# The first RMSNorm of a hybrid encoder block: sums of squares from a second copy of x with tokens on partitions

## The chip, the cores and the metric

The kernel runs on one core of one Trainium2 chip. The metric is the device time of one execution in microseconds (us): 740.09 us, the median of 3 runs (740.04 to 740.13).

The engines go by their names in the profile: PE multiplies matrices, DVE works elementwise along partitions, ACT computes scaled copies, squares and table functions, POOL does a little setup, SP issues nearly all DMA transfers. Each engine works through its own list of instructions in order and waits where an operand or a buffer is not ready.

## The reference

One block over x of 512 tokens by 1024 channels, all in float32:

```
h = rms_norm(x, g_mix)                       # x * rsqrt(mean(x*x, channels) + 1e-6) * g
[u_a | u_b | gates] = h @ w_in               # 1024 -> 1280 + 1024 + 2048
A = (RG-LRU forward + backward of conv4(u_a)) @ p_a
B = (multi-scale mean pooling of u_b, per-group linear, scale) @ p_b
x = x + (sigmoid(g_a) * A + sigmoid(g_b) * B) @ w_out
up = conv3(rms_norm(x, g_ffn) @ w_up);  x = x + (gelu(gate) * val) @ w_down
out = rms_norm(x, g_final)
```

The change concerns only the first line: the factor 1/sqrt(mean of squares + eps) of each token.

## The kernel before

Activations lie with channels on the 128 partitions and the 512 tokens along the row, so x is fetched as eight tiles xt of 128 x 512 from a transposed copy xT. Each matrix product runs in three passes: weights and activations are split into a high part hi and a low part lo, and `mm` (lines 211 to 218) issues hi by hi, hi by low activations and low weights by hi: lines 216, 217 and 218 in the profile.

The weights come in chunks of eight 128 x 128 blocks (512 KB), in the order in which PE reads them. `need` (line 199) sees to it that chunk c is fetched (`fetch`, line 181, on SP) and cut (`cut`, line 189: the high half on ACT, line 192, the low half on DVE, line 193). There are four buffers each for the raw chunk, for its high half and for its low half, so a chunk waits for the chunk four places before it.

In the start stage PE works on the first seven output blocks of w_in at once, in seven PSUM banks st0 to st6: for each k of eight channel tiles it goes over the seven banks. Chunks 0 to 6 serve this stage; the last block of k = 6 is the first of chunk 6. The gain g_mix is multiplied in when x is split (line 226), and the token's factor 1/rms is applied to the finished products: every evacuation of a bank multiplies by the tile rstd1 (`evac`, line 361), in which all 128 partitions hold the same row of 512 factors.

The row comes about like this. ACT squares the eight xt tiles (`square`, line 326), DVE adds them up to ssq, still with channels on partitions. ssq is split, and `row_rstd` (line 232) multiplies it on PE by a matrix of ones: two matmuls (lines 235 and 236) behind k = 5, which sum over the partitions and leave the sum in each of them. ACT takes the square root (line 238) and DVE the reciprocal (line 239) of a 128 x 512 tile. The second norm uses the same helper.

In this stage the order on ACT, DVE and SP is that of the code (`pin` keeps it); PE's order, and what follows the stage, is set by a scheduler. Transfers on SP wait in order: at most eight are under way at a time, since each waits for the one eight places before it.

Of the kernel before, what the change touches and what calls it, by code (L numbers as in the profile page):

```python
# [9 lines left out]
F32 = mybir.dt.float32  # L10
F32R = mybir.dt.float32r
AF = mybir.ActivationFunctionType
ALU = mybir.AluOpType

P = 128
S = 512
D = 1024
KD = D // P
# [110 lines left out]


@with_exitstack
def block_kernel(ctx: ExitStack, tc: tile.TileContext, xT, fst, wts, cst, gfin, out):
    nc = tc.nc
    cp = ctx.enter_context(tc.tile_pool(name="cp", bufs=1))
    wp = ctx.enter_context(tc.tile_pool(name="wp", bufs=1))
# [3 lines left out]
    dp = ctx.enter_context(tc.tile_pool(name="dp", bufs=1, space=bass.MemoryType.DRAM))  # L139
# [4 lines left out]
    def T(dt=F32, name="t"):  # L144
        seq[0] += 1
        return up.tile([P, S], dt, tag="T", name=f"{name}_{seq[0]}", bufs=59)
# [5 lines left out]
    def PS(name="ps"):  # L152
        seq[0] += 1
        return psp.tile([P, S], F32, tag="ps", name=f"{name}_{seq[0]}", bufs=8)
# [3 lines left out]
    rstd1 = cp.tile([P, S], F32, tag="rstd", name="rstd1", bufs=1)  # L158
    eps = cp.tile([P, 1], F32, name="eps")
# [15 lines left out]
    ve = Pinned()  # L175

    def pin(ins):
        if pinned[0]:
            tc.keep_in_program_order(ins)

    def fetch(c):
        raws[c] = wp.tile([P, UNITS * P], F32, tag="raw", name=f"raw_{c}", bufs=4)
        pin(nc.sync.dma_start(raws[c], wts[c]))
# [5 lines left out]
    def cut(c):  # L189
        raw = raws.pop(c)  # L190
        halves(c)
        pin(nc.scalar.activation(his[c], raw, AF.Copy))  # L192
        pin(nc.vector.tensor_tensor(los[c], raw, his[c], op=ALU.subtract))  # L193
# [4 lines left out]
    def need(c, ahead=AHEAD):  # L198
        while fetched[0] < min(NCHUNK, c + 1 + ahead):
            fetch(fetched[0])  # L200
            fetched[0] += 1
        while ready[0] < min(NCHUNK, c + 1 + ahead):
            cut(ready[0])
            ready[0] += 1

    def unit(u):
        c, i = divmod(POS[u], UNITS)
        need(c, AHEAD if c >= NST else 0)
        s = slice(i * P, (i + 1) * P)
        return his[c][:, s], los[c][:, s]  # L210

    def mm(ps, u, x, start, stop, cols=slice(0, S)):
        wh, wl = unit(u)
        xh, xl = x[0][:, cols], x[1][:, cols]
        o = ps[:, cols]
        nc.tensor.matmul(o, wh, xh, start=start, stop=False)  # L216
        nc.tensor.matmul(o, wh, xl, start=False, stop=False)  # L217
        nc.tensor.matmul(o, wl, xh, start=False, stop=stop)  # L218

    def split(t, name, g=None):  # L220
        hi, lo = T(F32R, name + "h"), T(F32R, name + "l")
        if g is None:
            pin(nc.scalar.activation(hi, t, AF.Copy))
            pin(nc.vector.tensor_tensor(lo, t, hi, op=ALU.subtract))
        else:
            pin(nc.scalar.activation(hi, t, AF.Copy, scale=g))
            pin(nc.vector.scalar_tensor_tensor(
                lo, in0=t, scalar=g, in1=hi.bitcast(F32), op0=ALU.mult, op1=ALU.subtract
            ))
        return hi, lo  # L230

    def row_rstd(ssq, rstd, halves=None):
        ps = PS("ssq")
        hi, lo = halves or split(ssq, "ssq")
        nc.tensor.matmul(ps, onesr, hi, start=True, stop=False)
        nc.tensor.matmul(ps, onesr, lo, start=False, stop=True)
        std = T(F32, "std")
        nc.scalar.activation(std, ps, AF.Sqrt, scale=1.0 / D, bias=eps)
        nc.vector.reciprocal(rstd, std)

    FU = 2
    FW = FU * P
    first = T(F32, "first")
    xts = [T(F32, "xt") for _ in range(KD)]
# [13 lines left out]
    def gmix(k):  # L258
        return first[:, FW + k : FW + k + 1]

    def start_cut():
        halves(0)
        hi, lo, raw = his[0], los[0], raws.pop(0)
        xh, xl = T(F32R, "xh"), T(F32R, "xl")
        f, h = slice(0, FW), S // 2
        ve.tensor_copy(hi[:, f], first[:, f])
        pin(nc.scalar.activation(xh[:, 0:h], xts[0][:, 0:h], AF.Copy, scale=gmix(0)))
        ve.tensor_scalar(xh[:, h:S], xts[0][:, h:S], gmix(0), None, op0=ALU.mult)
        ve.tensor_tensor(lo[:, f], first[:, f], hi[:, f], op=ALU.subtract)
        ve.scalar_tensor_tensor(  # L270
            xl, in0=xts[0], scalar=gmix(0), in1=xh.bitcast(F32), op0=ALU.mult, op1=ALU.subtract
        )
        for s in rest:
            pin(nc.scalar.activation(hi[:, s], raw[:, s], AF.Copy))
            ve.tensor_tensor(lo[:, s], raw[:, s], hi[:, s], op=ALU.subtract)
        return xh, xl
# [7 lines left out]
    def derived():  # L284
        for dst, n, w in ((hbg, "b_gate", 16), (hbx[:, 0:NH], "bx_f", NH), (hbx[:, NH:], "bx_b", NH)):
            c = COLS[n]
            ve.tensor_scalar(dst, consts[:, c : c + w], 0.5, None, op0=ALU.mult)
        lam = consts[:, COLS["lam_f"] : COLS["lam_f"] + 20]
        tmp = [cp.tile([P, 20], F32, name=f"tmp{i}") for i in range(5)]
        ab, ee, zz, z2, acc = tmp  # L290
        ve.tensor_scalar(ab, lam, -1.0, None, op0=ALU.mult)
        ve.tensor_tensor(ab, ab, lam, op=ALU.max)
        pin(nc.scalar.activation(ee, ab, AF.Exp, scale=-1.0))
        ve.tensor_scalar(zz, ee, 2.0, None, op0=ALU.add)
        ve.reciprocal(zz, zz)
        ve.tensor_tensor(zz, zz, ee, op=ALU.mult)
        ve.tensor_tensor(z2, zz, zz, op=ALU.mult)
        ve.memset(acc, 1.0 / 17.0)
        for n in (15, 13, 11, 9, 7, 5, 3, 1):
            ve.tensor_tensor(acc, acc, z2, op=ALU.mult)  # L300
            ve.tensor_scalar(acc, acc, 1.0 / n, None, op0=ALU.add)
        ve.tensor_tensor(acc, acc, zz, op=ALU.mult)
        ve.tensor_scalar(ab, lam, -1.0, 0.0, op0=ALU.mult, op1=ALU.max)
        ve.scalar_tensor_tensor(acc, in0=acc, scalar=2.0, in1=ab, op0=ALU.mult, op1=ALU.add)
        ve.tensor_scalar(c4, acc, 4.0, None, op0=ALU.mult)
        ve.tensor_scalar(c8n, acc, -8.0, None, op0=ALU.mult)
        ve.tensor_tensor(
            bps, consts[:, COLS["b_pool"] : COLS["b_pool"] + 8],
            consts[:, COLS["pool_scale"] : COLS["pool_scale"] + 8], op=ALU.mult,
        )  # L310
# [10 lines left out]
            pin(nc.sync.dma_start(consts, cst))  # L321
    fetched[0] = 4
    ready[0] = 1
    ssq = T(F32, "ssq")

    def square(k):
        sq = ssq if k == 0 else T(F32, "sq")
        pin(nc.scalar.activation(sq, xts[k], AF.Square))
        if k:
            ve.tensor_tensor(ssq, ssq, sq, op=ALU.add)  # L330

    for k in range(KD):
        xs.append(split(xts[k], "x", gmix(k)) if k else start_cut())
        if 0 < k < 4:
            need(k, 0)
        if k > 1:
            square(k - 2)
    square(KD - 2)
    square(KD - 1)
    ssqs = split(ssq, "ssq")  # L340
    for k in range(KD):
        need(min(k, NST - 1), 0)
        if k == KD - 2:
            derived()
        for m in range(NST):
            if k:
                mm(banks[m], ("w_in", k, m), xs[k], False, k == KD - 1)
        if k == 0:
            hi, lo = xs[0]
            for ms, parts in (((0, 1), (0, 2, 1)), ((2, 3), (0, 1, 2)), ((4, 5, 6), (0, 1, 2))):  # L350
                for part in parts:
                    for m in ms:
                        w = unit(("w_in", 0, m))[part == 2]
                        nc.tensor.matmul(
                            banks[m], w, lo if part == 1 else hi, start=part == 0, stop=False
                        )
        if k == KD - 3:
            row_rstd(ssq, rstd1, ssqs)
    pinned[0] = False

    def evac(ps, name):
# [410 lines left out]
```

## Time and profile before

| | |
|---|---|
| median of 3 runs | 740.09 us |
| the profiled execution | 740.16 us |
| its span, first to last instruction | 738.4 us |
| busy: PE, DVE, ACT, POOL | 729.3, 497.8, 364.6, 12.7 us |
| granted clock of PE, mean | 0.998 of full speed |
| DMA over the span | 81.46 MB, 110 GB/s |

Times in rows are counted from the start of the span. A row of the timeline gives the start, the time, the engine, the line, the operation with its tiles, and in brackets how long the engine had stood idle and for whom. PE's matmuls overlap: each is shown at about 0.39 us, and a new one starts every 0.23 us. SPq and ACTq rows are the issue of a transfer, not the transfer.

### The profile page before, as it was taken

The page shows a single profiled execution, that of the slowest core. Times are in us where ns is not written, and L with a number is a line of the kernel's source. Part 1 is how long each engine was busy: PE and PEld are TensorE (multiplying, and loading weights), DVE is VectorE, ACT ScalarE, POOL GpSimd, SP SyncE. Part 2 cuts the span into 40 slices and gives each one's busy share as a digit, 9 for nine tenths or more (in the row PEclk, how much of TensorE's full clock was granted, in tenths as well). Part 3 has the DMA queues.
Part 4 walks back from the last instruction along what each step waited for, and adds up shares of the span by engine and source line. Part 5 has one row for each costly group of instructions (what it writes and reads, how often), then busy time and mean ns, then how long its engine had stood idle before and what let it go on. Part 6 is the DMA issues. An engine that isn't in the chain of part 4 may idle for free.

```text
span 738.4 us, 8293 instructions
## 1 busy us (share of the span) xinstructions
PE 729.3 (99%) x3204; PEld 600.3 (81%) x3204; DVE 497.8 (67%) x665; ACT 364.6 (49%) x480; POOL 12.7 (2%) x19
## 2 busy tenths in 40 slices
PE   9999999999999999999999999999999999999996
PEld 6888888778888888888888888888888888888885
DVE  6495998968788779581544999877323677775215
ACT  7332389587777796232434745444221344443224
POOL 0000000000000000000130000000000000000000
PEclk9999999999999999999999999999999999999999
DMA  9242320423223223323442144555322323223103
GB/s 343 66 169 88 110 91 29 143 86 115 86 85 115 87 84 102 127 99 115 143 155 87 55 158 156 140 159 132 113 86 87 113 87 111 89 92 136 58 1 114
DMA packets 41415, 81.46 MB, mean 110 GB/s; under 512 B 19616, under 2 KB 20000, under 8 KB 41376
## 3 DMA queue, kind: packets, MB, share of 16 engines
q1 hardware_dynamic: 40656, 79.75, 33.2%
q10 hardware_dynamic: 720, 1.18, 0.4%
q8 instruction: 25, 0.41, 0.2%
q14 instruction: 14, 0.11, 0.1%
HBM read 76.73 MB, written 4.19 MB: 110 GB/s over the span
## 4 chain that ended last, share of the span: by engine, by line
PE 94%; DVE 3%; ACT 1%; DMA 0%; issue 0%; DVEq 0%
PE up L217 11%; PE up L216 11%; PE up L218 11%; PE proj L216 6%; PE proj L218 6%; PE proj L217 6%; PE dn L625 5%; PE dn L627 5%; PE dn L626 5%; PE p_a L217 2%; PE p_a L216 2%; PE p_a L218 2%; PE pb L216 2%; PE pb L217 2%; PE w_out L217 2%; PE w_out L216 2%
## 5 line engine op out<-in xcount | busy, mean ns | idle before, releaser
L192 ACT ACTIVATE hi<-raw 128x1024 fp32r<-128x1024 f32 x132 | 139.0, 1058 | 201.9 <-PE dn L626 70.6
L193 DVE TENSOR_TENSOR lo<-raw,hi 128x1024 fp32r<-128x1024 f32 x132 | 160.8, 1219 | 112.9 <-ACT hi L192 112.2
L216 PE MATMUL proj<-xh,hi 128*128 128x512 f32 x216 | 84.0, 389 | 0.0
L218 PE MATMUL proj<-xh,lo 128*128 128x512 f32 x216 | 84.0, 389 | 0.0
L217 PE MATMUL proj<-xl,hi 128*128 128x512 f32 x216 | 84.0, 389 | 0.0
L374 DVE SCALAR_TENSOR_TENSOR fv<-fu,consts,fv 128x511 f32<-128x511 f32 x88 | 64.8, 745 | 1.4 <-ACT fv L368 0.3
L594 DVE TENSOR_TENSOR fu<-up,rstd 128x512 f32<-128x512 f32 x44 | 29.9, 685 | 29.0 <-PE up L218 28.9
L218 PEld LDWEIGHTS proj<-xh,lo 128*128 128x128 f32 x216 | 40.5, 188 | 8.5
L217 PEld LDWEIGHTS proj<-xl,hi 128*128 128x128 f32 x216 | 40.5, 188 | 8.4
L216 PEld LDWEIGHTS proj<-xh,hi 128*128 128x128 f32 x216 | 40.5, 188 | 8.3
L368 ACT ACTIVATE fv<-fu,consts 128x512 f32<-128x512 f32 x44 | 35.3, 809 | 7.0 <-DVE fu L594 6.6
L596 ACT ACTIVATE fv<-fv 128x512 f32<-128x512 f32 x22 | 13.9, 631 | 33.7 <-DVE fv L374 33.7
L216 PE MATMUL pb<-poh,hi 128*128 128x512 f32 x64 | 25.0, 391 | 0.0
L217 PE MATMUL pb<-pol,hi 128*128 128x512 f32 x64 | 24.9, 390 | 0.0
L218 PE MATMUL pb<-poh,lo 128*128 128x512 f32 x64 | 24.9, 389 | 0.0
L423 DVE SCALAR_TENSOR_TENSOR s<-r,s 128x1024 f32<-128x1024 f32 x10 | 12.2, 1219 | 17.8 <-ACT s L414 17.8
L374 DVE SCALAR_TENSOR_TENSOR xa<-ua,consts,xa 128x511 f32<-128x511 f32 (+1 forms) x30 | 22.3, 744 | 0.3
L216 PE MATMUL st<-xh,hi 128*128 128x512 f32 x49 | 19.1, 389 | 0.0
L217 PE MATMUL st<-xl,hi 128*128 128x512 f32 x49 | 19.1, 389 | 0.0
L585 POOL TENSOR_TENSOR ssq<-ssq,sq 128x512 f32<-128x512 f32 x7 | 11.9, 1693 | 379.0 <-ACT sq L583 379.0
L218 PE MATMUL st<-xh,lo 128*128 128x512 f32 x49 | 18.3, 389 | 0.0
L217 PE MATMUL up<-x1g7l,hi 128*128 128x512 f32 x44 | 17.2, 392 | 0.0
(800 smaller groups left out, 1759.4 us busy)
## 6 DMA issues: line engine op xcount, KB each, us to landing
raw<-wts SPq DMA_DIRECT2D x132, 512.0 KB, 3.3
xt<-xT SPq DMA_DIRECT2D x8, 256.0 KB, 6.3
xr<-xT SPq DMA_DIRECT2D x8, 256.0 KB, 3.6
x1d<-tr SPq DMA_DIRECT2D x8, 256.0 KB, 2.2
x1t<-x1d SPq DMA_DIRECT2D x32, 64.0 KB, 2.8
out<-y SPq DMA_DIRECT2D x4, 256.0 KB, 2.1
out<-y ACTq DMA_DIRECT2D x4, 256.0 KB, 2.5
gf<-gfin SPq DMA_DIRECT2D x2, 256.0 KB, 4.0
```

The costliest lines, as they stand in the source:

```text
L192: pin(nc.scalar.activation(his[c], raw, AF.Copy))
L193: pin(nc.vector.tensor_tensor(los[c], raw, his[c], op=ALU.subtract))
L216: nc.tensor.matmul(o, wh, xh, start=start, stop=False)
L217: nc.tensor.matmul(o, wh, xl, start=False, stop=False)
L218: nc.tensor.matmul(o, wl, xh, start=False, stop=stop)
L368: nc.scalar.activation(dst, src, AF.Identity, scale=col(wn, left * nt + i), bias=col(bn, i))
L374: nc.vector.scalar_tensor_tensor(dst[:, a:b], in0=src[:, a + o : b + o], scalar=col(wn, k * nt + i), in1=dst[:, a:b], op0=ALU.mult, op1=AL ...
L594: nc.vector.tensor_tensor(u[:, n, :], ps, rstd2, op=ALU.mult)
L596: nc.scalar.activation(v[:, 0, :], v[:, 0, :], AF.Gelu_apprx_tanh)
L625: nc.tensor.matmul(ps, ah, his[c][:, s], start=start, stop=False)
L626: nc.tensor.matmul(ps, al, his[c][:, s], start=False, stop=False)
L627: nc.tensor.matmul(ps, ah, los[c][:, s], start=False, stop=stop)
```

## The change

x is passed to the kernel once more, as it is (xn, 512 x 1024, tokens first). Eight tiles of 128 tokens by 512 channels are fetched behind weight chunk 5. ACT squares each and sums along the row in the same instruction, which gives eight columns of sums; DVE adds the two columns that belong to the same 128 tokens; ACT and DVE take the square root and the reciprocal of a 128 x 4 tile. This tile is written to a row of 512 numbers in device memory, and a second transfer reads that row into all 128 partitions of rstd1. Chunks 4 and 5 are now cut ahead of the squares. The squares of xt, their sum, the split and the two matmuls are gone.

```diff
-    def row_rstd(ssq, rstd, halves=None):
+    def row_rstd(ssq, rstd):
         ps = PS("ssq")
-        hi, lo = halves or split(ssq, "ssq")
+        hi, lo = split(ssq, "ssq")
...
+    def row_sent(sums, rstd):
+        tot = cp.tile([P, 4], F32, name="tot")
+        ve.tensor_tensor(tot, sums[:, 0:4], sums[:, 4:8], op=ALU.add)
+        pin(nc.scalar.activation(tot, tot, AF.Sqrt, scale=1.0 / D, bias=eps))
+        ve.reciprocal(tot, tot)
+        row = dp.tile([4, P], F32, name="row")
+        pin(nc.sync.dma_start(row.rearrange("t p -> p t"), tot))
+        a = row[:, :]
+        pin(nc.sync.dma_start(rstd, bass.AP(a.tensor, a.offset, [[0, P], [1, S]])))
...
-    ssq = T(F32, "ssq")
-
-    def square(k):
-        sq = ssq if k == 0 else T(F32, "sq")
-        pin(nc.scalar.activation(sq, xts[k], AF.Square))
-        if k:
-            ve.tensor_tensor(ssq, ssq, sq, op=ALU.add)
-
     for k in range(KD):
         xs.append(split(xts[k], "x", gmix(k)) if k else start_cut())
         if 0 < k < 4:
             need(k, 0)
-        if k > 1:
-            square(k - 2)
-    square(KD - 2)
-    square(KD - 1)
-    ssqs = split(ssq, "ssq")
+    need(5, 0)
+    sums1 = cp.tile([P, 8], F32, name="sums1")
+    xns = [T(F32, "xn") for _ in range(8)]
+    for i in range(8):
+        h, t = divmod(i, 4)
+        pin(nc.sync.dma_start(xns[i], xn[t * P : (t + 1) * P, h * S : (h + 1) * S]))
+    for i in range(8):
+        pin(nc.scalar.activation(T(F32, "sq"), xns[i], AF.Square, accum_out=sums1[:, i : i + 1]))
+    row_sent(sums1, rstd1)
...
-        if k == KD - 3:
-            row_rstd(ssq, rstd1, ssqs)
```

On SP, behind the last fetch of an xt tile (raw_4 is the buffer of weight chunk 4 and so on, xt_9 the last tile of x), there stood before:

```order
L317 DMA xt_9_89<-xT 128x512
L183 DMA raw_4_298<-wts 128x1024
L183 DMA raw_5_325<-wts 128x1024
L183 DMA raw_6_358<-wts 128x1024
L183 DMA raw_7_470<-wts 128x1024
L183 DMA raw_8_472<-wts 128x1024
```

and now stand there, with six more fetches of xn between the two shown:

```order
L183 DMA raw_4_187<-wts 128x1024
L183 DMA raw_5_189<-wts 128x1024
L343 DMA xn_34_200<-xn 128x512
...
L343 DMA xn_41_207<-xn 128x512
L247 DMA row_236<-tot_232 128x4x1
L249 DMA rstd1_77<-row_236 128x512
L183 DMA raw_6_365<-wts 128x1024
L183 DMA raw_7_477<-wts 128x1024
```

Chunks 6 and 7 moved behind ten transfers, of which the last two wait for the computed row.

On ACT, from the split of the last x tile (xh) on; hi_4 is the high half of chunk 4. Before:

```order
L226 ACTIVATE xh_37_197<-xt_9_89,first_1_81 128x512
L328 ACTIVATE sq_39_201<-xt_7_87 128x512
L328 ACTIVATE sq_40_204<-xt_8_88 128x512
L328 ACTIVATE sq_41_207<-xt_9_89 128x512
L223 ACTIVATE ssqh_42_210<-ssq_18_134 128x512
L192 ACTIVATE hi_4_300<-raw_4_298 128x1024
L192 ACTIVATE hi_5_327<-raw_5_325 128x1024
L238 ACT_TABLE_LOAD
L238 ACTIVATE std_45_355<-ssq_44_352,eps_78 128x512
L192 ACTIVATE hi_6_360<-raw_6_358 128x1024
```

Now, with six more squares between the two shown:

```order
L226 ACTIVATE xh_32_183<-xt_9_89,first_1_81 128x512
L192 ACTIVATE hi_4_191<-raw_4_187 128x1024
L192 ACTIVATE hi_5_195<-raw_5_189 128x1024
L345 ACTIVATE sq_42_216,sums1_199<-xn_34_200 128x512
...
L345 ACTIVATE sq_49_230,sums1_199<-xn_41_207 128x512
L244 ACT_TABLE_LOAD
L244 ACTIVATE tot_232<-tot_232,eps_78 128x4
L192 ACTIVATE hi_6_367<-raw_6_365 128x1024
```

The cuts of chunks 4 and 5 moved ahead of the squares, and the square root no longer waits for a product of PE.

On PE, the last bank (st6) at k = 6, the first that reads chunk 6. Before:

```order
L217 MATMUL st5_16_118<-xl_35_191,hi_5_327 128x512
L218 MATMUL st5_16_118<-xh_34_190,lo_5_328 128x512
L216 MATMUL st6_17_119<-xh_34_190,hi_6_360 128x512
L217 MATMUL st6_17_119<-xl_35_191,hi_6_360 128x512
L216 MATMUL st0_11_113<-xh_37_197,hi_6_360 128x512
```

Now:

```order
L218 MATMUL st5_16_118<-xh_30_179,lo_5_196 128x512
L216 MATMUL st6_17_119<-xh_30_179,hi_6_367 128x512
L217 MATMUL st6_17_119<-xl_31_180,hi_6_367 128x512
L218 MATMUL st6_17_119<-xh_30_179,lo_6_368 128x512
L216 MATMUL st0_11_113<-xh_32_183,hi_6_367 128x512
```

The product with the low half of chunk 6 stood later before; now it is the third of its bank.

## Rows read from the trace of the kernel before

**Rows 1.** The page's busy line (part 1) and chain by engine (part 4).

```profile
PE 729.3 (99%) x3204; PEld 600.3 (81%) x3204; DVE 497.8 (67%) x665; ACT 364.6 (49%) x480; POOL 12.7 (2%) x19
...
PE 94%; DVE 3%; ACT 1%; DMA 0%; issue 0%; DVEq 0%
```

**Rows 2.** PE's waits over the span: us in total, times, longest.

```profile
PE hr2f L217 <- DVE xa2l L224: 1.1, 1, 1.1
...
PE st L354 <- DVE xh L173: 0.5, 1, 0.5
```

**Rows 3.** Timeline (start us, us) at 112 to 146 us: ACT, DVE, PE.

```profile
112.44 0.69 ACT L395 ACTIVATE r<-hr1f,consts 128x512 f32<-128x512 f32 x1 [2.05 <-PE hr1f L218]
...
122.46 1.23 DVE L423 SCALAR_TENSOR_TENSOR s<-r,s 128x1024 f32<-128x1024 f32 x1 [3.39 <-ACT s L414]
...
143.00 0.50 PE L217 MATMUL hr2f<-xa2l,hi 128*128 128x512 f32 x1 [1.13 <-DVE xa2l L224]
```

**Rows 4.** Timeline of PE around the norm's matmuls, and at 38 us.

```profile
33.55 0.39 PE L235 MATMUL ssq<-ssqh,onesr 128*128 128x512 f32 x1
33.78 0.40 PE L236 MATMUL ssq<-ssql,onesr 128*128 128x512 f32 x1
34.01 0.40 PE L216 MATMUL st<-xh,hi 128*128 128x512 f32 x1
...
38.12 0.39 PE L216 MATMUL st<-xh,hi 128*128 128x512 f32 x1
```

**Rows 5.** Timeline of DVE, 34 to 42 us.

```profile
34.94 3.35 DVE L239 RECIPROCAL rstd<-std 128x512 f32<-128x512 f32 x1 [9.29 <-ACT std L238]
...
38.20 1.16 DVE L193 TENSOR_TENSOR lo<-raw,hi 128x1024 fp32r<-128x1024 f32 x1
...
41.50 1.89 DVE L363 TENSOR_TENSOR ua<-st,rstd 128x512 f32<-128x512 f32 x3 [0.61 <-PE st L218]
```

**Rows 6.** Timeline of SP: the fetches of chunks 6 and 7.

```profile
12.01 0.33 SPq L183 DMA_DIRECT2D raw<-wts  x1
...
14.40 0.33 SPq L183 DMA_DIRECT2D raw<-wts  x1
```

**Rows 7.** Windows of the start stage (last two columns: DMA share, GB/s).

```profile
15.00:19.00 4.00, 4.00 (x19) 3.33 (x18) 4.00 (x7) 4.00 (x8) 0.00 (x0) 1.00 0.99 394
19.00:22.00 3.00, 3.00 (x15) 2.46 (x14) 2.42 (x4) 0.56 (x2) 0.00 (x0) 1.00 0.03 8
```

**Rows 8.** Timeline of ACT: the cut of one weight chunk's high half.

```profile
38.10 1.06 ACT L192 ACTIVATE hi<-raw 128x1024 fp32r<-128x1024 f32 x1 [0.35 <-PE st L217]
```

**Rows 9.** The tile x1t: squares with a sum (ns min/median/max).

```profile
L679 ACT ACTIVATE sq<-x1t x8: 629/633/635, 718.2 to 732.5; 128x512 f32<-128x512 f32 x8
L679 ACT ACTIVATION_READ_ACCUMULATOR sq<-x1t x8: 184/186/188, 718.8 to 733.1; 128x1 f32 x8
```

**Rows 10.** Timeline of ACT at 116 us: a table load and what follows.

```profile
116.21 1.28 ACT L410 ACT_TABLE_LOAD   x1
117.51 2.57 ACT L410 ACTIVATE r<-r,c8n 128x512 f32<-128x512 f32 x4
```

**Rows 11.** Timeline at 733 us: square root and reciprocal of one column.

```profile
733.28 0.29 ACT L681 ACTIVATE fin<-fin 128x1 f32<-128x1 f32 x1
733.60 0.16 DVE L173 RECIPROCAL fin<-fin 128x1 f32<-128x1 f32 x1 [0.51 <-ACT fin L681]
```

**Rows 12.** The tile x1t: its copies from issue to landing.

```profile
DMA to landing us min/median/max: 2.2/2.8/4.9
```

**Rows 13.** The page's DMA issues (part 6): KB each, us to landing.

```profile
raw<-wts SPq DMA_DIRECT2D x132, 512.0 KB, 3.3
...
xr<-xT SPq DMA_DIRECT2D x8, 256.0 KB, 3.6
x1d<-tr SPq DMA_DIRECT2D x8, 256.0 KB, 2.2
```

**Rows 14.** DMA queues, 498 to 503 us: packets, MB, share of 16 engines.

```profile
q1 hardware_dynamic: 5386, 0.67, 87.1%
```

More of the change, by code (lines that the diff above doesn't have):

```diff
@@ L131, in block_kernel @@
 @with_exitstack
-def block_kernel(ctx: ExitStack, tc: tile.TileContext, xT, fst, wts, cst, gfin, out):
+def block_kernel(ctx: ExitStack, tc: tile.TileContext, xT, xn, fst, wts, cst, gfin, out):
     nc = tc.nc
@@ L761 @@
     gfin = np.ascontiguousarray(np.broadcast_to(np.asarray(g_final), (P, D)))
-    arrays = {"xT": xT, "fst": np.ascontiguousarray(fst), "wts": wts, "cst": cst, "gfin": gfin}
+    xn = np.ascontiguousarray(np.asarray(x)[0])
+    arrays = {"xT": xT, "xn": xn, "fst": np.ascontiguousarray(fst), "wts": wts, "cst": cst, "gfin": gfin}
     args = [
```

## The prediction, made before the changed kernel had run

> **What bounds the kernel now.** I read first the page's busy line and its chain: PE is busy for 729.3 us of the 738.4 us span, and 94% of the chain that ended last is PE [rows 1]. The reader is to see that only what removes matmuls, or stops PE, can move the end. Then I looked for where PE stands still. Between its first real matmul and its last there is one wait worth naming, 1.13 us at 143.00 us, in front of head 2's second matmul, for the low half that DVE makes [rows 2, 3]. In the stretch that the change touches, the first 50 us, PE runs through: one matmul starts every 0.23 us [rows 4], and nothing is gained by making ACT or DVE lighter there. So the question for this change is what PE loses or saves itself, and whether one of the operands it reads in the start stage now comes too late.
>
> What the norm costs PE now: two matmuls in mid stream, the first at 33.55 us, the next product at 34.01 us [rows 4]. The rest of it stands beside PE. The factors are first used by DVE at 41.50 us, when the first bank is complete [rows 5]. The one place where the old norm made others late is DVE's reciprocal of a full tile, 3.35 us from 34.94 us, behind which the low half of weight chunk 6 waited until 38.20 us [rows 5]. PE had its products ordered around that and lost nothing.
>
> **Removed.** (1) PE: the two ssq matmuls, 34.01 - 33.55 = 0.46 us, on the path, all of it saved. (2) ACT: eight squares of transposed tiles, one rounding of the sums and a square root over a full tile; DVE: seven adds, one subtraction and the 3.35 us reciprocal. All lie beside PE, which waits for none of them, so I count zero.
>
> **Added and moved.** The chain of the new norm is long, and what matters is who is queued behind it. SP issues the eight fetches of xn where it issued chunks 6 and 7 (at 12.01 and 14.40 us [rows 6]); then the write of the row, which waits for DVE's small reciprocal; then the copy to all partitions, which waits for that write to land; and only then chunk 6, then 7, 8 and 9. PE's first product with chunk 6 is the seventh bank's at k = 6: 38.12 us before [rows 4], so 37.66 us now, and by the new order the third product of that bank, with the low half, follows 0.46 us later, at 38.12 us. That is the deadline that decides. The working:
>
> - Transfers: the DMA engines run full, 394 GB/s from 15 to 19 us, and nearly stop behind that, 8 GB/s [rows 7], so what stood in the queue before had landed by about 19.0 us. Now 8 x 0.262 = 2.10 MB of xn stand there instead of 2 x 0.524 = 1.05 MB of chunks 6 and 7. The extra 1.05 MB at 394 GB/s take 2.7 us: the last xn lands at 21.7 us, and the first, with 0.67 us for each, at about 17.0 us. Everything fetched ahead of them keeps its place.
> - ACT: the squares come behind the cuts of chunks 4 and 5. Chunk 5 has landed just before the first xn, at 16.3 us, so with 1.06 us for its cut [rows 8] ACT is free at 17.4 us. A square with a sum along the row is 0.63 us, and reading the sum 0.19 us [rows 9]: eight take at most 6.5 us, to 23.9 us.
> - Then the table load, 1.28 us with the sum of two columns beside it (to 25.2 us) [rows 10]; a square root of a few columns 0.29 us and a reciprocal of them 0.16 us [rows 11]: with 0.1 us for handing over, 25.7 us.
> - The write of the row: 512 pieces of 4 bytes to memory. No row shows one. The nearest in number of pieces is the x1t copy, 512 pieces of 128 bytes: 2.2 to 4.9 us, median 2.8 [rows 12]; the nearest in direction is the write x1d, 2.2 us [rows 13]. I take 2.8 us and keep 2.2 and 4.9 as ends: landed at 28.5 us.
> - The copy to all partitions, 256 KB: like xr, 3.6 us [rows 13], so the factors stand at about 32.2 us. DVE wants them at 41.50 - 0.46 = 41.04 us: 8.8 us to spare, which would cover three and a half such copies.
> - Chunk 6: issued at about 28.9 us, 3.3 us to land [rows 13], and 0.65 us more behind the copy's 0.26 MB: 32.8 us. High half 1.06 us, to 33.9 us; low half 1.16 us [rows 5, 8], to 35.1 us. Against 37.66 and 38.12 us that leaves 3.8 and 3.0 us.
>
> So the cover for the whole new chain is 3.0 us, and it is gone when the row's write takes over 2.8 + 3.0 = 5.8 us; beyond this each us of it is one us of the kernel. Both ends of the bound, 2.2 and 4.9 us, lie under that, so the term is zero at either end. Chunks 7 to 9 land at 1.3 us apiece behind chunk 6, and PE needs them 24 matmuls, 5.4 us, apart. The head-room below nothing: PE waits for nothing in this stretch, so a gain beyond 0.46 us has no place to come from there.
>
> [...] The trace shows a table load of 1.28 us at 116.21 us and the next activation at 117.51 us, with nothing between [rows 10]. [...]
>
> **What comes after the start stage.** Behind the evacuation of the last start bank each engine's order is the same as before, and each wait names the same engines. The one wait of PE, at 143.00 us, hangs on PE itself: ACT takes up head 1 at 112.44 us after standing idle 2.05 us for PE's hr1f product, and DVE takes up the result at 122.46 us after 3.39 us idle for ACT [rows 3]. From there DVE works through to the low half that PE waits for. So this wait moves forward with PE and keeps its length.
>
> **Sum.** The profiled execution took 740.16 us, with 738.4 us of span and 1.76 us around it. 740.16 - 0.46 + 0 = 739.70 us. It lies 0.07 us above the median of the runs, 740.09 us, so I forecast 739.63, say 739.6 us. What a measurement of this kernel can tell from no change I set at 0.2%, or 1.48 us: the forecast is no change by that measure.
>
> **Rivals.**
> *The row's write turns into PE's wait (slower).* Place: SP's queue between the row and chunk 6. It decides from 5.8 us for the write, costs more than the matmuls save from 5.8 + 0.46 = 6.3 us, and over 0.2% from 6.3 + 1.48 = 7.7 us. A mechanism that gets there: the 512 pieces go one behind another instead of side by side. In the stretch with only x1t copies moving, 5386 pieces took 87.1% of 16 engines' 5 us [rows 14], 16 x 5.0 x 0.871 / 5386 = 12.9 ns each; 512 of them in one line are 6.6 us, and with the 2.4 us of an x1t copy that are not its 32 pieces per engine, 9.0 us. PE then waits 9.0 - 5.8 = 3.2 us: 742.8 us. For it: nothing in this trace writes such small pieces to memory, and each could cost more than one that reads 128 bytes. Against it: the x1t copies, over 32 partitions, did spread over the engines, and the row lies over 128. [...] Chance 7%.
>
> *The 0.46 us do not arrive.* If part of the wait at 143.00 us were set by something that does not move with PE, the saving would be waited away there: 740.1 us. Against it stand the two idle gaps of [rows 3] that tie it to PE. A row's write of 6.3 us would give the same time. Chance 9%.
>
> *The wait of PE at 143.00 us goes too.* DVE loses its long reciprocal and does the small setup operations earlier; if that lead lasted to head 2, 1.13 us more would go: 739.63 - 1.13 = 738.5 us, just over 0.2% faster. Against it: DVE stands idle 3.39 us at 122.46 us, so no lead outlives that. Chance 3%.
>
> *The change does not do what it says*, because the factors reach the banks later than the old ones did: they would have to be 8.8 us later than worked out before the first bank waits, and PE comes back to that bank only after a whole projection. Then the same write is to blame, and chunk 6 has already stopped PE; it is inside the first rival.
>
> **Numbers.** Forecast 78%, the three rivals 7, 9 and 3%, and 3% for what I have not seen, a point of it on the faster and a point on the slower side. Faster by over 0.2%: 0.03 + 0.01 = 0.04; slower: 0.07 + 0.01 = 0.08; within: 0.88. The range holds the forecast and the case without gain, with some tenths for the wait at 143 us and for a write that just misses its cover: 739.0 to 740.6 us. The slower rival stays outside.
>
> **What would show it.** Right: no ssq matmul on PE; PE's list of waits with the 1.1 us for head 2 and nothing new in the first 50 us; the row landing in 2 to 5 us from 25.7 us on; chunk 6 issued near 29 us; ua0 waiting for PE's st and not for a DMA. Wrong: a PE wait on chunk 6's hi or lo near 38 us (then the row's landing time is the failed term), squares that end well behind 24 us (then the transfers), or a wait at 143 us of another length.

## The result, and the profile after

The changed kernel is 0.9% slower: 747.65 us, median of 6 runs (746.25 to 748.24), against 741.18 us (740.04 to 742.67) for the kernel before beside it. The ratio is 1.009, with an interval of 1.0078 to 1.0102. The profiled execution took 748.24 us, with 746.5 us of span; that is 8.08 us over the profiled execution of before, 740.16 us.

The page of the changed kernel, busy line and chain by engine, answers to [rows 1]:

```profile
PE 731.2 (98%) x3202; PEld 601.0 (81%) x3202; DVE 490.1 (66%) x658; ACT 364.9 (49%) x487; POOL 12.7 (2%) x19
...
PE 89%; DMA 5%; DVE 3%; ACT 2%; SPq 0%; issue 0%; DVEq 0%; ACTq 0%
```

Two matmuls fewer, and yet PE is busy 1.9 us longer. The chain that ended last now runs through DMA for 5% of the span, where it was 0%. PE's waits, as in [rows 2], say where:

```profile
PE st L216 <- ACT hi L192: 6.0, 1, 6.0
PE hr2f L217 <- DVE xa2l L224: 1.1, 1, 1.1
```

The wait for head 2 is what it was. New is one wait of 6.0 us in the start stage, for the high half of a weight chunk. The timeline of PE there, as in [rows 4] (start, us, engine, line, operation; in brackets the idle time before it and for whom):

```profile
37.18 0.39 PE L218 MATMUL st<-xh,lo 128*128 128x512 f32 x1
43.58 0.79 PE L216 MATMUL st<-xh,hi 128*128 128x512 f32 x1 [6.02 <-ACT hi L192]
44.17 0.63 PE L217 MATMUL st<-xl,hi 128*128 128x512 f32 x1
...
51.48 0.39 PE L216 MATMUL proj<-xh,hi 128*128 128x512 f32 x1
```

PE stands still for 6.02 us in front of the first product with chunk 6, and then its first products take 0.63 and 0.79 us instead of 0.39. From 43.58 to 51.48 us, where the next stage's first product starts, it does 24 products in 7.90 us; at the 0.227 us at which it starts one elsewhere that is 5.44 us. So 2.46 us more are lost behind the wait. Two things lie in them. One is the low half of the same chunk, which DVE makes: PE's load of its weights for the third product (PEld) waits for it, and the product starts only at 44.84 us.

```profile
44.84 0.28 PEld L218 LDWEIGHTS st<-xh,lo 128*128 128x128 f32 x1 [0.76 <-DVE lo L193]
```

The other shows in the windows of this stretch (third column from the end: the granted clock, as a share of full speed):

```profile
38.00:42.00 4.00, 0.00 (x0) 0.00 (x0) 0.00 (x0) 0.00 (x0) 0.00 (x0) 0.91 0.69 240
42.00:46.00 4.00, 2.38 (x5) 1.46 (x6) 2.40 (x7) 3.29 (x3) 0.00 (x0) 0.50 0.93 358
46.00:48.00 2.00, 2.00 (x7) 1.52 (x6) 1.86 (x8) 1.99 (x4) 0.00 (x0) 0.50 0.73 262
48.00:50.00 2.00, 2.00 (x10) 1.65 (x9) 1.90 (x6) 0.24 (x1) 0.00 (x0) 0.98 0.85 262
```

While PE stood, its granted clock fell to 0.50 of full speed, and it was back near 1.00 (0.98) only from 48 us on. The waits and the slow products together account for the difference of the two profiled executions: 6.02 + 2.46 - 0.46 (the two matmuls that are gone) = 8.02 us, of 8.08.

The chain of waits over the same stretch, in order of time, shows what PE waited for:

```profile
17.75 6.88 DMA xn<-xn
...
27.23 9.01 DMA row<-tot
...
36.68 5.69 DMA raw<-wts
...
42.47 1.06 ACT hi L192
```

The write of the row, 2 KB, takes 9.01 us until it counts as landed, and only then does SP issue the copy and chunk 6. What the DMA engines did in that time, from 27.2 to 36.3 us (40 equal slices; busy tenths, then the queue):

```profile
DMA  0000640000000000000000000000000000000000
...
q1 hardware_dynamic: 528, 0.00, 2.8%
```

All 512 pieces pass the engines in two slices, about 0.5 us; for the remaining 7.6 us the engines show nothing, and the write has still not landed. The transfers ahead of it answer to [rows 7]:

```profile
19.00:22.00 3.00, 3.00 (x15) 2.45 (x15) 1.16 (x1) 3.00 (x11) 0.00 (x0) 1.00 1.00 368
22.00:26.00 4.00, 4.00 (x19) 3.34 (x18) 0.16 (x1) 2.53 (x7) 0.00 (x0) 1.00 0.05 14
```

The traffic ends near 22 us, as was worked out, but the last tile of xn counts as landed only at 24.6 us.

### The profile page after: what moved, and what is told of

It is laid out like the page before. It is cut to its first block, busy times and chain, and to the rows that moved or that the text cites. A ratio compares the mean times of both kernels' runs of the same rounds, so it can differ in the third digit from the quotient of the medians.

```text
span 746.5 us, 8299 instructions
## 1 busy us (share of the span) xinstructions
PE 731.2 (98%) x3202; PEld 601.0 (81%) x3202; DVE 490.1 (66%) x658; ACT 364.9 (49%) x487; POOL 12.7 (2%) x19
## 4 chain that ended last, share of the span: by engine, by line
PE 89%; DMA 5%; DVE 3%; ACT 2%; SPq 0%; issue 0%; DVEq 0%; ACTq 0%
PE up L217 11%; PE up L218 11%; PE up L216 11%; PE proj L218 6%; PE proj L216 6%; PE proj L217 6%; PE dn L629 5%; PE dn L630 5%; PE dn L631 5%; PE p_a L218 2%; PE p_a L217 2%; PE p_a L216 2%; PE pb L216 2%; PE pb L218 2%; PE w_out L218 2%; PE w_out L217 2%
## 5 line engine op out<-in xcount | busy, mean ns | idle before, releaser
L598 DVE TENSOR_TENSOR fu<-up,rstd 128x512 f32<-128x512 f32 x44 | 29.8, 684 | 29.0 <-PE up L218 28.9
L218 PE MATMUL st<-xh,lo 128*128 128x512 f32 x49 | 19.9, 407 | 0.0
```

The lines of the kernel that those rows point to most:

```text
L598: nc.vector.tensor_tensor(u[:, n, :], ps, rstd2, op=ALU.mult)
```

## The experiments

Theory: the write of 512 pieces of 4 bytes is slow by itself, and it costs time because chunk 6 stands behind it on SP. The rivals: the fetches of xn or the traffic of the stage hold chunk 6 up; the pieces go one behind another through an engine; and, for the rest of the loss, something other than the clock.

**Chunks 6 and 7 ahead of the row's write (queue).**

```diff
         pin(nc.sync.dma_start(xns[i], xn[t * P : (t + 1) * P, h * S : (h + 1) * S]))
+    for c in (6, 7):
+        fetch(c)
+    fetched[0] = 8
     for i in range(8):
```

> The changed kernel, with chunks 6 and 7 fetched behind the xn fetches and ahead of the row's write. Theory A (the place in SP's queue): in the changed kernel PE waited 6.02 us for the high half of chunk 6, which SP could issue only at 36.68 us, after the write of the row had taken 9.0 us to land. With the chunks ahead of the write, chunk 6 lands near 26 us and PE does not wait in the start stage; the row's write still takes about 9 us, the factors come near 41 us, just when the first bank is complete. Time: 0.46 us under the kernel before, ratio 0.9994. Theory B (the 2.1 MB of xn, not the write, make the weights late): PE still waits some us for chunk 6 and the time stays 0.5 to 1% above before.

Measured: 740.44 us (739.76 to 741.05, 11 runs), against 740.31 for before beside it, a ratio of 0.9994 (0.9985 to 1.0003). The timeline of SP:

```profile
17.90 2.36 SPq L183 DMA_DIRECT2D raw<-wts  x4
25.16 0.38 SPq L247 DMA_DIRECT2D row<-tot  x1
27.67 0.34 SPq L183 DMA_DIRECT2D raw<-wts  x1
35.68 0.33 SPq L249 DMA_DIRECT2D rstd<-row  x1
```

Four chunks, 6 to 9, went out ahead of the write: the edit names 6 and 7, and the scheduler put 8 and 9 behind them. The write is as slow as ever, 10.5 us from 25.16 to the copy's issue at 35.68, but no weight waits behind it that PE wants soon. PE has no wait in this stage, and DVE's first use of the factors waits for PE and not for the copy:

```profile
40.71 1.89 DVE L370 TENSOR_TENSOR ua<-st,rstd 128x512 f32<-128x512 f32 x3 [0.60 <-PE st L218]
```

That was close: the copy, 4.9 us from 35.68 us on, had landed only some 0.1 us earlier. So the whole loss came from the place of chunk 6 behind the write. That the fetches of xn hold chunk 6 up falls: here it still stands behind all eight of them.

**The write as 128 pieces of 16 bytes (tok4).** Partition p now holds the tokens 4p to 4p + 3, so that its four factors lie next to each other in the row.

```diff
-        row = dp.tile([4, P], F32, name="row")
-        pin(nc.sync.dma_start(row.rearrange("t p -> p t"), tot))
+        row = dp.tile([P, 4], F32, name="row")
+        pin(nc.sync.dma_start(row, tot))
...
-        pin(nc.sync.dma_start(xns[i], xn[t * P : (t + 1) * P, h * S : (h + 1) * S]))
+        pin(nc.sync.dma_start(xns[i], xn.rearrange("(p t) d -> t p d", t=4)[t][:, h * S : (h + 1) * S]))
```

> The changed kernel, with another assignment of tokens to partitions: partition p holds tokens 4p to 4p+3, so that the row is written as 128 pieces of 16 bytes instead of 512 of 4 bytes; the queue is as in the changed kernel. In that kernel the engines moved the 512 pieces within some 0.5 us and then nothing moved for 7.6 us until the write counted as landed. Theory A1 (that silent time goes with the number of pieces): 7.6 / 4 = 1.9 us, the write lands after about 3.3 us, chunk 6 is issued near 31 us, PE does not wait, ratio 0.9994. Theory A2 (the silent time is the same for any write of small pieces to memory): the write takes about 9 us again, PE waits 6 us, ratio 1.009. Theory B (the 2.1 MB of xn): PE waits as in the changed kernel, whatever the write takes.

Measured: 740.47 us (739.55 to 742.19, 11 runs), a ratio of 1.0001 (0.9991 to 1.0011). The timeline of SP, with chunk 6 as the first of the eleven in the last row:

```profile
25.52 0.33 SPq L247 DMA_DIRECT2D row<-tot  x1
26.93 0.33 SPq L249 DMA_DIRECT2D rstd<-row  x1
27.35 29.95 SPq L183 DMA_DIRECT2D raw<-wts  x11
```

The order of the changed kernel is kept, and the write of the same 2 KB lands in 1.4 us instead of 9.0. Chunk 6 is cut from 33.37 us on and PE does not wait. So it is the form of the write; number and size of its pieces changed together here. Theory A1 had said 3.3 us: the silent time fell by more than the number of pieces did.

**Both edits (both).**

> Both edits together: chunks 6 and 7 ahead of the write, and the write as 128 pieces of 16 bytes. Theory A with A1 or A2: no wait of PE in the start stage, ratio 0.9994, the two matmuls of 0.46 us saved; with A1 the factors stand near 35 us, 6 us before the first bank is complete. Theory B: 0.5 to 1% above before.

Measured: 740.33 us (739.55 to 742.18, 11 runs), a ratio of 0.9998 (0.9989 to 1.0007). The two edits do not add up: either alone already frees PE. The write took 3.8 us here; weights were still moving when it was issued (344 to 475 GB/s in the slices from 24 to 26 us), but no run tests whether that is the reason.

**Products in place of the stand-still (filled).** In front of the first product with chunk 6, PE does 26 products whose result nothing uses.

```diff
+            if (k, m) == (6, 6):
+                for _ in range(26):
+                    nc.tensor.matmul(wps, his[5][:, 0:P], xs[5][0], start=True, stop=True)
```

> The changed kernel, with 26 products of old operands, 0.227 us each or 5.9 us in all, put on PE right before the product that waits 6.02 us for chunk 6; their result is used by nobody. In the changed kernel the granted clock was 0.50 from 42 to 48 us, and the 24 products from 43.58 to 51.48 us took 7.90 us instead of 24 x 0.227 = 5.44, so 2.46 us of the loss are put down to the clock after the wait. If that clock follows PE's standing still, the products behind chunk 6 start every 0.227 us, and the time is 2.46 us under the changed kernel, ratio to before 1.0075 where the changed kernel has 1.0105 by its profile. If the slow products had another cause (the transfers that run full at the same time), nothing changes: ratio 1.009 to 1.0105.

Measured: 746.42 us (746.18 to 747.65, 4 runs), a ratio of 1.0082 (1.0069 to 1.0096). The timeline of PE, from the fillers (line 354 here) on, and a window as above:

```profile
39.53 3.56 PE L354 MATMUL warm<-xh,hi 128*128 128x512 f32 x15
...
45.42 0.39 PE L216 MATMUL st<-xh,hi 128*128 128x512 f32 x1
...
50.86 0.39 PE L216 MATMUL proj<-xh,hi 128*128 128x512 f32 x1
...
42.00:46.00 4.00, 4.00 (x19) 3.31 (x18) 3.10 (x9) 3.76 (x5) 0.00 (x0) 1.00 0.85 323
```

The fillers hold PE for 45.42 - 39.53 = 5.89 us, nearly the 6.02 us of the changed kernel's wait, and the clock stays at 1.00. Now the same 24 products take 50.86 - 45.42 = 5.44 us instead of 7.90, though the DMA engines are nearly as busy as there (0.85 of their time from 42 to 46 us, against 0.93). So transfers are not what slows the products.

Not all of the 2.46 us is the clock, as the expectation had it. In the changed kernel the low half was ready at 44.79 us, so the third product could not have started sooner at any clock; up to its start, 44.84 - 43.58 - 2 x 0.227 = 0.81 us were lost. The 22 products from there to 51.48 us took 6.64 us instead of 4.99: 1.65 us are the clock's. In this run the low half was ready at 44.06 us, before the fillers ended, so it takes away both.

The time decides nothing: the ratio, 1.0082, lies between the two that were expected, and its interval overlaps that of the changed kernel, 1.009. The wait of the changed kernel is not the same in each execution (6.0, 5.3 and 4.9 us in its three profiles, the last two with test transfers behind its end), while the fillers always cost 5.9. In the execution shown PE came to the fillers 2.1 us later than it came to its wait in the changed kernel, and the high half was ready at 42.79 us: the wait would have been about 3.3 us. The reading rests on the timeline.

**What makes the write slow (probe).** Test transfers behind the last output, one after the other, with nothing else moving. The core of it:

```diff
+    packed = dp.tile([4, P], F32, name="packed")
+    pin(nc.sync.dma_start(packed.rearrange("t p -> p t"), q[:, 0:4]))
...
+    quads = dp.tile([P, 4], F32, name="quads")
+    pin(nc.sync.dma_start(quads, q[:, 0:4]))
...
+    lines = dp.tile([4, P, 16], F32, name="lines")
+    pin(nc.sync.dma_start(lines[:, :, 0:1].rearrange("t p o -> p t o"), q[:, 0:4].rearrange("p (t o) -> p t o", o=1)))
```

> The changed kernel, with test transfers behind its last output, one after the other, nothing else running: 512 pieces of 4 bytes next to each other as the row has them (packed, and again as a repeat), 128 pieces of 16 bytes (quads), 512 pieces of 4 bytes each 512 bytes from the next (apart) or 64 bytes from the next (lines), 1024 pieces next to each other (eight), 128 pieces of 4 bytes next to each other (single), and a whole tile of 256 KB; each is read back, packed, quads and again as one row of 2 KB into all 128 partitions. Only the times from issue to landing are of use.
>
> Theory A, the number of pieces decides: packed, apart and lines take the same, about 9 us; eight about 17 us; single, with as many pieces as quads, the same 1.4 us.
>
> Theory B, pieces that lie in the same short stretch of memory hold each other up: packed 9 us; eight longer; apart, where no two lie within 512 bytes, about as quads, 1.4 to 2.5 us; single longer than quads though it has the same 128 pieces; lines in between, which bounds the stretch.
>
> Theory C, something of the start stage (weights under way, a queue) made the write slow there: packed lands here in 2 to 3 us.
>
> The copies: if 128 partitions that read the same 2 KB make the copy slow, it takes 4 to 5 us here too and the read back of the whole tile, the same 256 KB from distinct places, 2.5 to 3.6 us; if it was the traffic of the start stage, both take the same.

Measured, in the DMA view's list of issues (KB each, median us from issue to landing):

```profile
q<-packed SPq DMA_DIRECT2D x1, 256.0 KB, 5.0
q<-quads SPq DMA_DIRECT2D x1, 256.0 KB, 3.5
...
q<-whole SPq DMA_DIRECT2D x1, 256.0 KB, 2.6
...
packed<-q SPq DMA_DIRECT2D x1, 2.0 KB, 9.2
quads<-q SPq DMA_DIRECT2D x1, 2.0 KB, 1.7
apart<-q SPq DMA_DIRECT2D x1, 2.0 KB, 1.8
...
lines<-q SPq DMA_DIRECT2D x1, 2.0 KB, 1.8
...
eight<-q SPq DMA_DIRECT2D x1, 4.0 KB, 8.7
...
single<-q SPq DMA_DIRECT2D x1, 0.5 KB, 7.5
```

Packed takes 9.2 us with nothing else moving, and 10.1 us when repeated, so the start stage is not to blame (theory C falls). The same 512 pieces take 1.8 us when they lie 64 or 512 bytes apart, and 128 pieces next to each other still take 7.5: the number does not decide (theory A falls), the neighbourhood does (theory B). Two parts of B are wrong: twice the pieces in twice the stretch, eight, take no longer, and lines came out like apart, not in between.

The copies came out between the two expectations. 128 partitions reading the same 2 KB take 3.5 to 5.0 us in three copies, distinct 256 KB 2.6 in one; so the common source costs about 1 to 2.4 us.

**The same in its place (spaced).** The row's 512 pieces go to places 64 bytes apart; all else is as in the changed kernel. The copy reads 2 KB of that place, so most of the factors are filler and the first norm is not computed.

```diff
+    spaced = dp.tile([4, P, 16], F32, name="spaced")
...
-        pin(nc.sync.dma_start(row.rearrange("t p -> p t"), tot))
-        a = row[:, :]
+        pin(nc.sync.dma_start(spaced[:, :, 0:1].rearrange("t p o -> p t o"), tot[:, :].rearrange("p (t o) -> p t o", o=1)))
+        a = spaced[:, :, :]
```

> The changed kernel with one thing other: the 512 pieces of 4 bytes go to places 64 bytes apart in device memory instead of next to each other. Same number, same size, same queue, same order of all engines. The copy behind it reads 2 KB from the start of that place, as before, so that it waits for the write and moves as much; but of those 512 numbers only 32 are factors, the rest is filler written there early by one 32 KB transfer, so the first norm is not computed here.
>
> Theory B (pieces in one short stretch of memory hold each other up): the write lands in 1.8 us instead of 9.0, as the test transfers 64 bytes apart did. Chunk 6 is then issued 7.2 us earlier, at about 29.5 us instead of 36.7, its high half is done near 36.4 us, before PE asks for it at about 37.5; PE waits for at most a few tenths of a us there, the clock stays at 1.00, and the kernel takes 740.4 us, the same as before the change within 0.2%.
>
> Theory A (the number of pieces decides) or C (the start stage makes the write slow): the write takes 9 us, PE waits 5 to 6 us for chunk 6, and the kernel takes about 747.5 us.

Measured: 740.10 us (739.62 to 741.01, 10 runs), against 740.57 for before beside it, a ratio of 0.9995 (0.9985 to 1.0005). SP's timeline:

```profile
25.35 0.38 SPq L249 DMA_DIRECT2D spaced<-tot  x1
27.13 0.34 SPq L254 DMA_DIRECT2D rstd<-spaced  x1
27.56 29.73 SPq L183 DMA_DIRECT2D raw<-wts  x11
```

1.8 us, and PE's wait is gone. Number, size and queue of the pieces and the order of the engines are as in the changed kernel; the distance between the pieces differs, and one transfer of 32 KB, the filler, goes out ahead of the xn fetches. Theory B holds in the kernel itself.

**How far apart is enough (stride).** More test transfers of the same kind: 512 pieces of 4 bytes at distances of 4 (packed, again), 8, 16, 32 and 64 bytes, then pairs of 8 bytes, quads and far.

```diff
+    by8 = dp.tile([4, P, 2], F32, name="by8")
+    pin(nc.sync.dma_start(by8[:, :, 0:1].rearrange("t p o -> p t o"), one(4)))
```

> The changed kernel, with a second row of test transfers behind its last output, one after the other: 512 pieces of 4 bytes next to each other (packed, again), and 8, 16, 32 and 64 bytes from one to the next (by8, by16, by32, by64); 256 pieces of 8 bytes next to each other (pairs); 128 pieces of 16 bytes next to each other (quads) and 512 bytes apart (far). Only the times from issue to landing are of use.
>
> Theory B1, each piece waits its turn within a stretch of 64 bytes: the landing falls in proportion to the pieces in 64 bytes: packed (16 pieces) 9 us, by8 and pairs (8 pieces) about 5 us, by16 and quads (4) about 2 to 3 us, by32 (2) and by64 (1) 1.8 us, far as quads or 0.2 us shorter.
>
> Theory B2, the stretch is shorter, 32 bytes: packed has 8 pieces in it, by8 and pairs 4, by16 and quads 2, by32 and by64 1: by32 equals by64, and by16 equals quads.
>
> Theory B3, a threshold in the size of a piece and not its neighbours: pieces of 4 bytes are slow whenever another lies within 64 bytes (by8, by16, by32 all about 9 us) and pieces of 8 and 16 bytes are not (pairs and quads 1.7 us).

Measured, on SP's timeline. Each transfer waits for the one before it, so its time is the next start less its own; the four rows `by<-q` are 8, 16, 32 and 64 bytes:

```profile
742.48 0.38 SPq L715 DMA_DIRECT2D packed<-q  x1
752.09 0.38 SPq L716 DMA_DIRECT2D q<-packed  x1
755.87 0.36 SPq L718 DMA_DIRECT2D by<-q  x1
760.33 0.36 SPq L719 DMA_DIRECT2D q<-by  x1
762.29 0.36 SPq L721 DMA_DIRECT2D by<-q  x1
765.00 0.36 SPq L722 DMA_DIRECT2D q<-by  x1
766.80 0.36 SPq L724 DMA_DIRECT2D by<-q  x1
768.88 0.36 SPq L725 DMA_DIRECT2D q<-by  x1
770.69 0.36 SPq L727 DMA_DIRECT2D by<-q  x1
772.77 0.36 SPq L728 DMA_DIRECT2D q<-by  x1
```

And two more from the list of issues (KB, us from issue to landing):

```profile
quads<-q SPq DMA_DIRECT2D x1, 2.0 KB, 1.4
far<-q SPq DMA_DIRECT2D x1, 2.0 KB, 1.4
```

9.6 us packed (10.9 when repeated), then 4.5, 2.7, 2.1 and 2.1 us. Over the 2.1 us without neighbours the excess is 7.5, 2.4, 0.6 and 0 us: each of the first two doublings of the distance takes away some 70% of it, where theory B1 said half. Pairs of 8 bytes took 3.1 us (B1 said about 5), quads 1.4, far 1.4. B3 falls, since 8 and 16 bytes apart are not as slow as packed. That 32 equals 64 bytes speaks for the shorter stretch of B2, that quads and 16 bytes apart differ speaks against it, though quads also has a quarter of the pieces; and quads lose nothing by lying next to each other, since far is as fast. Which stretch the pieces share stays open. What goes on in it stays open too; the trace shows only when a write counts as landed.

## Why the prediction was wrong

The failed step is one term of the sum, "The write of the row: 512 pieces of 4 bytes to memory", taken as 2.8 us with ends of 2.2 and 4.9 us. It measured 9.0 us, beyond the break-even of 5.8 us that the prediction had worked out itself. Both neighbours were the wrong kind: x1t has 512 pieces, but of 128 bytes and on the way in [rows 12]; x1d is a write, but of whole rows [rows 13]. Neither has small pieces that lie close together in memory, so the ends of the bound bounded something else, and "the term is zero at either end" did not follow.

- **Removed:** the two ssq matmuls are gone from PE, as forecast. Whether their 0.46 us (0.06%) arrive can't be told: the four kernels in which PE does not wait have ratios of 0.9994, 1.0001, 0.9998 and 0.9995, all with 1 inside their intervals.
- **Transfers:** the traffic ended near 22 us, but the last xn landed at 24.6 instead of 21.7 us, so the squares ended late and the row's write was issued at 27.2 instead of 25.7 us: 1.5 us of the cover gone.
- **ACT and DVE:** durations as taken from rows of before: squares 0.63, table load 1.28, square root 0.30, reciprocal 0.18 us. The square root follows the table load as closely as in [rows 10]: the load of 1.28 us starts at 25.39 us, the square root at 26.69.
- **The row's write:** 6.2 us over the value taken.
- **The copy:** 4.8 instead of 3.6 us, and covered. The prediction's 8.8 us to spare would hold 2.4 further copies, not three and a half; nothing hangs on it.
- **Chunk 6:** issued at 36.7 instead of 28.9 us (1.5 + 6.2 us), landed after 5.7 instead of 3.95 us, behind a copy that reads one 2 KB row 128 times. Its high half was ready 9.6 us later than forecast; 3.8 us of that were covered; the rest, 5.8 us, is PE's wait but for 0.2 us by which this execution had started earlier. The low half, which the prediction rightly called the deadline that decides, was ready at 44.79 instead of 35.1 us: 9.7 us late, of which 3.0 were covered. The late xn and chunk 6's slower landing alone, 1.5 + 1.75 us, already use up these 3.0 us, so the write's 6.2 us reached PE in full.
- **The clock:** not priced at all. "Beyond this each us of it is one us of the kernel" was wrong: the wait of 6.02 us for the high half cost 8.48, of which 0.81 went to the low half and 1.65 to the clock.
- **After the start stage:** right. The wait for head 2 kept its 1.1 us [rows 2], PE's list has no other new wait, and 8.02 of the 8.08 us arise in the start stage.

The rival "the row's write turns into PE's wait" named the place, the queue and even the 9.0 us, but the 9.0 us were luck, for its mechanism was wrong: the pieces did not go one behind another through an engine. They passed in 0.5 us, and 512 of them land in 1.8 us when spaced. Its 742.8 us were too low by the late xn (1.5 us), by chunk 6's slower landing (1.75 us) and by the clock (1.65 us). How far apart such pieces must lie, the runs bound from above: at 64 bytes they were as fast as at 512, 1.8 us in probe.

## What to carry to other kernels

A write of a column layout to a row in memory is cheap in bytes and can still take 9 us to land, as the 512 pieces of 4 bytes from 128 partitions, next to each other, did here (9.0 us in the changed kernel); give each partition a piece of its own of 16 bytes, as tok4 did (1.4 us). Fetch what the engine needs next ahead of a transfer that waits for a computed value: the queue behind it waits as well, as chunk 6 did, issued at 36.68 us behind a write issued at 27.23. And price a new stall of PE above its length, since the clock may come back later than PE does: here PE went on at 43.58 us and the clock was at 0.50 until 48 us, which cost 1.65 us.

## What the runs showed of the hardware

- The time until a write counts as landed can be far longer than the time its pieces take on the DMA engines: 9.0 us against 0.5 us.
- 128, 512 and 1024 pieces of 4 bytes, packed, landed after 7.5, 9.2 and 8.7 us (512 when repeated: 9.6 to 10.9): the time hardly depends on the number.
- A copy in which all partitions read the same 2 KB ran at half the rate of one from distinct places. The DMA view's GB/s, in slices of 0.25 us, of probe from 790 to 800 us (whole written from 794 us, read back from 796 us) and from 750 to 760 us (the copy of the row, from 755 us):

```profile
GB/s 0 0 0 0 0 0 0 0 0 0 0 1 0 0 0 0 57 377 393 221 0 0 0 0 0 66 0 131 426 377 49 0 0 0 0 2 6 0 0 0
```

```profile
GB/s 0 0 0 0 0 0 0 0 0 0 0 0 0 0 0 0 0 0 0 0 0 131 172 180 188 148 180 49 0 0 0 0 8 0 0 0 0 0 0 0
```
